# One quarter of each weight's small part, formed by an accumulating DMA in SBUF instead of a VectorE subtraction

## The chip, the cores and the metric

The kernel runs on one core of a Trainium2 chip. The time is device microseconds of that core for one execution. TensorE does the matrix products, VectorE (DVE in the rows) and ScalarE (ACT) the elementwise work, GpSimd (POOL) small chains of arithmetic, and 16 DMA engines move data; transfers are issued from the queues of SyncE (SP) and, in a few places, of GpSimd.

## The reference

Two decoder layers for 256 tokens of width 2048, in float32. Each layer is a token mixer (pooling in layer 0, sparse attention with an indexer in layer 1), a cross attention over 256 memory tokens, and a SwiGLU block; a last norm follows. What matters here is that nearly all the work is products of a [256, 2048]-like operand with weights that are read once:

```python
for i in range(DEPTH):
    x = x + mixer(rms_norm(x, norm_mix[i]))                      # pooling, or q/k/v/indexer and output products
    x = x + memory_cross_attention(rms_norm(x, norm_xattn[i]), memn, xattn_w_q[i], xattn_w_kv[i], xattn_w_o[i])
    x = x + swiglu(rms_norm(x, norm_ffn[i]), ffn_w_in[i], ffn_w_out[i])
return rms_norm(x, norm_final)

def swiglu(h, w_in, w_out):                                      # w_in 2048 x 11264, w_out 5632 x 2048
    g, u = jnp.split(h @ w_in, 2, axis=-1)
    return (jax.nn.silu(g) * u) @ w_out
```

## The kernel before, in words

**Pieces.** All weights are cut into 344 pieces of 128 partitions x 2048 columns (four of 1344), listed in `pieces` in the order in which the products use them. A piece is loaded from HBM into a `raw` tile (`load_to`, L139, on SP's queue, 1 MB), and then split into a large part `wh` and a small part `wl`, both in float32r, so that a float32 product becomes three products: `mm3` (L306 to L308) adds x_hi\*wh, x_hi\*wl and x_lo\*wh, and `mm_T` (L331, L332) is the same for results that are wanted transposed. There are three `raw` tiles and three tiles each of `wh` and `wl`.

**The split.** `split_unit` does the next 512 columns of the next piece: ScalarE copies them to `wh` with rounding (L154), and VectorE subtracts, `wl = raw - wh` (L155). A piece is thus four such units (three for the short ones).

**The order.** The program's order is written out by the code as it runs: between groups of six products the code calls `hook()`, which runs a job that is due and one or two split units. A piece may be split when at most two pieces before it are still in use (`state["cur"] + W_BUFS`), so in the steady state piece i + 2 is split while piece i is multiplied, into the tiles that piece i - 1 has just given back. The load of piece i + 2 is issued at the first split of piece i, and has to wait until the `raw` tile that it goes into has been read by the last split of piece i - 1.

**Who waits for whom.** ScalarE's first L154 of a piece waits for TensorE's last L308 of the piece three before it. L155 waits for L154. TensorE's L306 waits for L154 and L307 for L155. SP's L139 waits for the last L155 of the piece that had the tile. GpSimd has little to do: the inverse square roots of the norms (L270 to L273, seven chains of twelve instructions), six additions in the pooling mixer (L520), and the one transfer that it issues (L915).

Of the kernel before, what the change touches and what calls it, by code (L numbers as in the profile page):

```python
# [34 lines left out]
GROUPS = ((0, 4), (4, 8), (8, 11))  # L35
# pieces of the output product of the sparse attention: those of the last heads come late
AO_ORDER = [(n, j) for j in range(4) for n in range(2)] + [(n, j) for n in (2, 3) for j in range(4)]
# [3 lines left out]
NINF = -1.0e30  # L41
# 2*pi in three parts; the first two have few bits, so their multiples are exact
TPI = (6.28125, 0.0019340515136718750, 1.2556656679e-06)

# when work between products is due, in hooks: what it reads has to be there by then, or the products wait
MIX_FIRST, MIX_SPREAD = 13, 22
X_SCORES, X_SPREAD, X_MIX, X_MIX_LAST = (2, 1), (7, 5, 4, 4), 2, 5
MEM_ROW, SQ_X = 24, 12
NORM_CHUNK, NORM_POOL = (2, 3, 5), (2, 0)
RAW_BUFS, W_BUFS, BIG_BUFS, TMP_BUFS = 3, 3, 12, 8  # L50


@with_exitstack
def trunk_kernel(ctx: ExitStack, tc: tile.TileContext, a: dict, out: bass.AP):
# [20 lines left out]
    def tmp(n=512):  # L75
        """Scratch of up to 512 columns."""
        return work.tile([P, 512], F32, tag="tmp", name="tmp", bufs=TMP_BUFS)[:, :n]
# [3 lines left out]

    # ---------------------------------------------------------------- weights
    pieces = []
# [59 lines left out]
    def split_unit():  # L143
        """The next columns of the next piece, in two parts."""
        i = state["split"]
        if i >= min(len(pieces), state["cur"] + W_BUFS):
            return
        load_to(i + RAW_BUFS)
        t, w, done = raws[i]
        if not done:  # L150
            parts[i] = tuple(wpool.tile([P, 2048], F32R, tag=n, name=n) for n in ("wh", "wl"))
        c = slice(len(done) * UNIT, min((len(done) + 1) * UNIT, w))
        wh, wl = parts[i]
        A.activation(wh[:, c], t[:, c], AF.Copy)  # L154
        V.tensor_tensor(wl[:, c], t[:, c], wh[:, c].bitcast(F32), op=ALU.subtract)  # L155
        done.append(c)
        if c.stop == w:
            raws.pop(i)
            state["split"] += 1
# [11 lines left out]

    # ------------------------------------------------- work put between matmuls
    jobs, side = deque(), deque()
    made = set()

    def job(fn, delay=1, key=None):
        """fn is run by a hook, the first one that comes ``delay`` hooks from now or later and after the jobs before it."""
        jobs.append((state["hook"] + delay, fn, key))
# [7 lines left out]
    def hook():  # L186
        """Between products: a job that is due, and the next columns of weights."""
        if jobs and jobs[0][0] <= state["hook"]:
            run_job()
        if side and state["hook"] % 3 < 2:  # L190
            side.popleft()()
        split_unit()
        if state["split"] <= state["cur"] + 1:
            split_unit()
        state["hook"] += 1
# [4 lines left out]

    # -------------------------------------------------------------- constants
    gains = const.tile([P, 6, KT], F32, name="gains")
# [37 lines left out]

    # ------------------------------------------------------------------ norms
    def sumsq(dst, src, on_v=False):
# [8 lines left out]
    def rstd_of(sums, E=V, dst=None):  # L251
        """1/sqrt(sum/D + eps) of each [P, 4] of partial sums, in float32: [P, len(sums)]."""
        n = len(sums)
# [26 lines left out]

    # ------------------------------------------- transposed operands, in parts
    def split_psum(dst_h, dst_l, src):
# [11 lines left out]
    def transpose_pair(dst, src_of, kt0, gi):  # L294
        """Two k-tiles of the stationary operand: dst[:, kt % 4, hi 256 | lo 256]."""
        tp = tp_tile()
        for u in range(2):
            for t in range(2):
                T.transpose(tp[:, (2 * u + t) * P:(2 * u + t + 1) * P], src_of(kt0 + u, t), ident)  # L299
        split_pair(dst, tp, kt0, gi)  # L300

    def mm3(acc, xt, k, t, wh, wl, c0, w, first, last):
        """acc += x[:, t].T @ W for one k-tile, as hi*hi + hi*lo + lo*hi."""
        xh = xt[:, k, t * P:(t + 1) * P]
        xl = xt[:, k, S + t * P:S + (t + 1) * P]
        T.matmul(acc[:, :w], lhsT=xh, rhs=wh[:, c0:c0 + w], start=first, stop=False)  # L306
        T.matmul(acc[:, :w], lhsT=xh, rhs=wl[:, c0:c0 + w], start=False, stop=False)  # L307
        T.matmul(acc[:, :w], lhsT=xl, rhs=wh[:, c0:c0 + w], start=False, stop=last)  # L308
# [5 lines left out]
    def gemm(keys, xs, name, w=512, acc=None, at=0):  # L314
        """One chunk of w columns; xs(j) gives the four k-tiles of piece j."""
        acc = acc or [acc_tile(), acc_tile()]
# [12 lines left out]
    def mm_T(acc, wh, wl, c0, xt, k, first, last):  # L329
        """acc += (128 columns of W).T @ [x hi | x lo] for one k-tile; lo * hi goes to the half of the small terms."""  # L330
        T.matmul(acc, lhsT=wh[:, c0:c0 + P], rhs=xt[:, k, :], start=first, stop=False)  # L331
        T.matmul(acc[:, S:2 * S], lhsT=wl[:, c0:c0 + P], rhs=xt[:, k, 0:S], start=False, stop=last)  # L332

    def gemm_T(key, xs):
        """A 128-column chunk with its result transposed: [128 columns, 256 tokens] and the small terms."""
        acc = acc_tile()
        wh, wl = w_get(key)
        for kt in range(KT):
            xt = xs(kt // 4)
            mm_T(acc, wh, wl, kt * P, xt, kt % 4, kt == 0, kt == KT - 1)  # L340
            if kt % 4 == 3 and kt < KT - 1:
                hook()
        return acc
# [6 lines left out]
    class Normed:  # L350
        """x as the stationary operand of the next products: x * gain, transposed, in parts; rstd apart."""

# [5 lines left out]
        def chunk(self, n, later=0):  # L358
            """Columns 512 n of x are final."""
            def pair(u):  # L360
# [25 lines left out]

    # ------------------------------------------------- memory keys and values
    # the memory transposed, as the moving operand of k and the stationary one of v; its tokens' factors come after
    ms, mem_r, kT, vm = {}, {}, {}, {}
# [14 lines left out]
    def squares(ss, src, c):  # L404
        """Two chunks of a token half, one by each of two engines."""
        def fn():
# [13 lines left out]
    def mem_row():  # L420
        """The factors of the memory's tokens as a row, on all partitions."""
        rb = tmp(S)
# [59 lines left out]

    # ------------------------------------------------------------ pooling mixer
    # x^T times a band matrix: row t' of it holds rstd[t'] times the weight of token t' in each token's difference
    diffs = {}
# [38 lines left out]

    # --------------------------------------------------- memory cross attention
    XSC = HD ** -0.5
# [100 lines left out]

    # ------------------------------------------------------------------- SwiGLU
    def ffn(L, xn, nxt):
# [32 lines left out]
        for gi, (t0, t1) in enumerate(GROUPS):  # L662
# [3 lines left out]
            for n in range(4):  # L666
                keys = [("fo", L, ht, n) for ht in range(t0, t1)]
                if last and n == 3 and isinstance(nxt, Final):
                    # one half of the tokens after the other: the first half's end runs under the second's products
                    for t in range(2):  # L670
# [16 lines left out]

    # ------------------------------------------------------- rotary tables
    rot = big_tile(F32, (P, 2048))
# [30 lines left out]

    # --------------------------------------------------------- sparse attention
    ASC = HD ** -0.5

    def rope(dst, src, t, nh, d, rtab):
        """dst = rotated src * rstd, [P, nh * d]; the tables hold rstd."""
        c0 = 0 if d == HD else 256
# [12 lines left out]
    def sparse(xn, nxt):  # L739
# [33 lines left out]
        def to_T(dst, q0, src, key):  # L773
            """The 4 x 128 columns of src[t], transposed to dst[:, q0 + i, 256 tokens]."""
            for i in range(0, 4, 2):
# [131 lines left out]

    # ------------------------------------------------------------------ layers
    class Final:
        """The last norm: x * gain as the chunks come, the factor of each token at the end."""  # L910

# [36 lines left out]

# ------------------------------------------------------------- layout on the host
def _consts():  # L950
# [15 lines left out]
def _rows(w, n):  # L966
    """[K, N] -> [n chunks of columns, K/512, 128, 4 * N/n]: what one load brings, by partition."""
    K, N = w.shape
# [3 lines left out]
def _cols(w):  # L972
    """[2048, 512] -> [4, 128, 16 * 128]: chunks of 128 columns."""
    return w.reshape(KT, P, 4, P).transpose(2, 1, 0, 3).reshape(4, P, KT * P)
# [45 lines left out]
```

## Time and profile before

| | |
|---|---|
| time, median of 2 runs | 2006.95 us (2006.17 and 2007.72) |
| profiled execution, first to last instruction | 2005.6 us; so some 1.4 us of the median lie around it |
| TensorE: products busy / weight loads busy | 1988.5 us (99%) / 1653.2 us (82%) |
| VectorE busy | 1164.4 us (58%), 871.1 of it L155 |
| ScalarE busy | 965.5 us (48%), 768.3 of it L154 |
| GpSimd busy | 37.7 us (2%) |
| mean granted TensorE clock | 0.999 |
| DMA | 370.03 MB, SP's queue busy for 51.3% of the 16 engines' span |

The page gives no time of its own for the profiled execution beside its span of 2005.6 us; that span stands 0.07% below the median of the runs. A product's busy time is modelled and products overlap, so 99% says that TensorE always had a product in flight, not how fast they followed each other; the pitch between the starts of successive products says that. Idle time of an engine is put down to what ended last before it went on.

### The profile page before, as it was taken

The numbers are of one execution on the slowest core, as the hardware profiler recorded it, in microseconds if no ns is written. First come the engines' busy times: TensorE is split into PE (matmuls) and PEld (weight loads), VectorE is DVE, ScalarE is ACT, GpSimd is POOL, SyncE is SP. The second block draws the span as 40 slices with busy tenths as digits, with TensorE's granted clock in tenths as the row PEclk, the third lists the DMA queues.
The fourth block names the chain that finished last, engine by engine and source line by source line (L and its number), as shares of the span: only waits on it lengthen the run. The fifth ranks groups of instructions, "written<-read, shape, count | busy, mean of one in ns | idle before, by whom it ended". The sixth has DMA issues, their size and how long they took to land.

```text
span 2005.6 us, 24311 instructions
## 1 busy us (share of the span) xinstructions
PE 1988.5 (99%) x9206; PEld 1653.2 (82%) x9206; DVE 1164.4 (58%) x2217; ACT 965.5 (48%) x1936; POOL 37.7 (2%) x98
## 2 busy tenths in 40 slices
PE   8999999999999999999999999999999999999998
PEld 7888888888888888888788888888888888888886
DVE  6766655554555555556687766755555555555555
ACT  6655544444444444455455555644443444444443
POOL 1100100000000000000000000000000000000000
PEclk9999999999999999999999999999999999999999
DMA  8344555555455545545544354554555555455552
GB/s 325 142 158 170 200 197 189 175 206 196 178 189 202 195 173 194 202 168 181 170 145 168 131 188 164 189 189 173 198 197 188 189 199 191 177 207 192 189 183 111
DMA packets 53974, 370.03 MB, mean 185 GB/s; under 512 B 6368, under 2 KB 7008, under 8 KB 10208
## 3 DMA queue, kind: packets, MB, share of 16 engines
q1 hardware_dynamic: 53712, 367.43, 51.3%
q8 instruction: 72, 1.18, 0.2%
q0 software_dynamic: 144, 1.05, 0.1%
q14 instruction: 46, 0.38, 0.1%
HBM read 366.36 MB, written 2.10 MB: 184 GB/s over the span
## 4 chain that ended last, share of the span: by engine, by line
PE 99%; ACT 0%; DMA 0%; DVE 0%; issue 0%; SPq 0%; ACTq 0%
PE acc L306 29%; PE acc L308 29%; PE acc L307 29%; PE acc L331 3%; PE acc L332 1%; PE tp L299 1%; PE tp L649 1%; PE sm L794 1%; PE sm L306 0%; PE sm L307 0%; PE sm L308 0%; PE sm L838 0%; PE sm L866 0%; PE sm L574 0%; PE sm L537 0%; PE tp L858 0%
## 5 line engine op out<-in xcount | busy, mean ns | idle before, releaser
L155 DVE TENSOR_TENSOR wl<-raw,wh 128x512 fp32r<-128x512 f32 x1372 | 871.1, 687 | 473.8 <-ACT wh L154 470.2
L154 ACT ACTIVATE wh<-raw 128x512 fp32r<-128x512 f32 x1372 | 768.3, 622 | 624.0 <-PE acc L308 610.7
L306 PE MATMUL acc<-wh,big 128*128 128x512 f32 x2592 | 1027.3, 396 | 0.0
L308 PE MATMUL acc<-wh,big 128*128 128x512 f32 x2592 | 1008.4, 389 | 0.0
L307 PE MATMUL acc<-wl,big 128*128 128x512 f32 x2592 | 1006.9, 388 | 0.0
L308 PEld LDWEIGHTS acc<-wh,big 128*128 128x128 f32 x2592 | 486.4, 188 | 102.0 <-DVE big L284 0.3
L307 PEld LDWEIGHTS acc<-wl,big 128*128 128x128 f32 x2592 | 487.2, 188 | 97.4 <-DVE wl L155 1.9
L306 PEld LDWEIGHTS acc<-wh,big 128*128 128x128 f32 x2592 | 486.9, 188 | 97.1 <-issue 1.9
L639 DVE SCALAR_TENSOR_TENSOR tmp<-acc,rs,sg 128x256 f32<-128x256 f32 x88 | 42.4, 483 | 128.7 <-ACT sg L638 128.7
L638 ACT ACTIVATE sg<-acc,rs 128x256 f32<-128x256 f32 x88 | 41.6, 475 | 138.2 <-PE acc L308 138.2
L331 PE MATMUL acc<-big,wh 128*128 128x512 f32 x256 | 96.9, 417 | 1.4 <-DVE big L292 1.4
L385 DVE TENSOR_TENSOR x<-acc,x 128x512 f32<-128x512 f32 x70 | 47.4, 689 | 61.4 <-PE acc L308 61.4
L332 PE MATMUL acc<-big,wl 128*128 128x256 f32 x256 | 72.6, 284 | 0.1
L284 DVE TENSOR_TENSOR big<-tp,big 128x512 fp32r<-128x512 f32 x44 | 30.4, 692 | 62.6 <-ACT big L283 62.6
L283 ACT ACTIVATE big<-tp 128x512 fp32r<-128x512 f32 x44 | 26.3, 598 | 70.3 <-PE tp L649 70.3
L331 PEld LDWEIGHTS acc<-big,wh 128*128 128x128 f32 x256 | 49.0, 191 | 12.6 <-ACT wh L154 1.2
L292 DVE SCALAR_TENSOR_TENSOR big<-tp,gains,big 128x256 fp32r<-128x256 f32 x96 | 41.9, 478 | 26.3 <-ACT big L290 25.6
L290 ACT ACTIVATE big<-tp,gains 128x256 fp32r<-128x256 f32 x96 | 40.3, 475 | 34.3 <-PE tp L299 22.3
L332 PEld LDWEIGHTS acc<-big,wl 128*128 128x128 f32 x256 | 49.2, 192 | 1.0 <-DVE wl L155 0.6
L249 ACT ACTIVATE junk<-x 128x512 f32<-128x512 f32 x52 | 33.1, 637 | 20.5 <-DVE x L385 11.4
L847 ACT ACTIVATE tmp<-tmp,mx 128x128 f32<-128x128 f32 (+1 forms) x32 | 14.3, 448 | 40.2 <-DVE mx L845 40.2
L270 POOL TENSOR_TENSOR rs<-rs 128x2 f32<-128x2 f32 x21 | 8.3, 396 | 1198.7 <-DVE rs L265 1197.6
(143 smaller groups left out, 621.1 us busy)
## 6 DMA issues: line engine op xcount, KB each, us to landing
raw<-in_fi SPq DMA_DIRECT2D x176, 1024.0 KB, 4.8
raw<-in_fo SPq DMA_DIRECT2D x88, 1024.0 KB, 4.8
raw<-in_wq SPq DMA_DIRECT2D x16, 1024.0 KB, 4.9
raw<-in_wao SPq DMA_DIRECT2D x16, 1024.0 KB, 4.9
raw<-in_xv SPq DMA_DIRECT2D x8, 1024.0 KB, 5.4
raw<-in_xq SPq DMA_DIRECT2D x8, 1024.0 KB, 4.7
raw<-in_xo SPq DMA_DIRECT2D x8, 1024.0 KB, 4.7
raw<-in_wqi SPq DMA_DIRECT2D x8, 1024.0 KB, 4.9
```

The costliest lines, as they stand in the source:

```text
L154: A.activation(wh[:, c], t[:, c], AF.Copy)
L155: V.tensor_tensor(wl[:, c], t[:, c], wh[:, c].bitcast(F32), op=ALU.subtract)
L290: A.activation(dst_h, src, AF.Copy, scale=g)
L292: V.scalar_tensor_tensor(dst_l, src, g, dst_h.bitcast(F32), op0=ALU.mult, op1=ALU.subtract)
L306: T.matmul(acc[:, :w], lhsT=xh, rhs=wh[:, c0:c0 + w], start=first, stop=False)
L307: T.matmul(acc[:, :w], lhsT=xh, rhs=wl[:, c0:c0 + w], start=False, stop=False)
L308: T.matmul(acc[:, :w], lhsT=xl, rhs=wh[:, c0:c0 + w], start=False, stop=last)
L331: T.matmul(acc, lhsT=wh[:, c0:c0 + P], rhs=xt[:, k, :], start=first, stop=False)
L332: T.matmul(acc[:, S:2 * S], lhsT=wl[:, c0:c0 + P], rhs=xt[:, k, 0:S], start=False, stop=last)
L385: V.tensor_tensor(xc, acc[t], xc, op=ALU.add)
L638: A.activation(sg, acc[t][:, 0:S], AF.Silu, scale=r[:, t:t + 1])
L639: V.scalar_tensor_tensor(h[:, t, :], acc[t][:, S:2 * S], r[:, t:t + 1], sg, op0=ALU.mult, op1=ALU.mult)
```

## The change

For every piece from the 13th on (`BY_DMA_FROM = 12`), the first unit of 512 columns no longer goes through VectorE. ScalarE writes `wh` as before and then a second time from `raw` into `wl`, with the sign turned (so `wl = -wh`); then GpSimd issues a transfer from `raw` to `wl` in SBUF that adds what it reads to what is there, so that `wl = raw - wh`. The other units, and the first twelve pieces, are as before. The line numbers of the changed kernel are higher by two before this place and by seven after it (L139 is L141, L306 to L308 are L313 to L315, L332 is L339). Other lines of the diff take comments away.

```diff
+BY_DMA_FROM = 12
...
         A.activation(wh[:, c], t[:, c], AF.Copy)
-        V.tensor_tensor(wl[:, c], t[:, c], wh[:, c].bitcast(F32), op=ALU.subtract)
+        if len(done) == 0 and i >= BY_DMA_FROM:
+
+            A.activation(wl[:, c], t[:, c], AF.Copy, scale=-1.0)
+            nc.gpsimd.dma_start(wl[:, c], t[:, c], accum_op=ALU.add)
+        else:
+            V.tensor_tensor(wl[:, c], t[:, c], wh[:, c].bitcast(F32), op=ALU.subtract)
```

ScalarE, in the first SwiGLU block, around one pair of activations (`sg`) and the split of a result (`big`). Before:

```order
L638 ACTIVATE sg<-acc,rs 128x256 x2
L154 ACTIVATE wh<-raw 128x512 x2
L283 ACTIVATE big<-tp 128x2x256
L154 ACTIVATE wh<-raw 128x512 x14
L638 ACTIVATE sg<-acc,rs 128x256 x2
```

The same place with the change:

```order
L645 ACTIVATE sg<-acc,rs 128x256 x2
L156 ACTIVATE wh<-raw 128x512 x2
L159 ACTIVATE wl<-raw 128x512
L290 ACTIVATE big<-tp 128x2x256
L156 ACTIVATE wh<-raw 128x512 x4
L159 ACTIVATE wl<-raw 128x512
L156 ACTIVATE wh<-raw 128x512 x4
L159 ACTIVATE wl<-raw 128x512
L156 ACTIVATE wh<-raw 128x512 x4
L159 ACTIVATE wl<-raw 128x512
L156 ACTIVATE wh<-raw 128x512 x2
L645 ACTIVATE sg<-acc,rs 128x256 x2
```

Sixteen copies of ScalarE between two pairs of activations become twenty: one more behind the first unit of each piece, ahead of the other three.

GpSimd, at the end of the norm ahead of that block and behind it, with what each instruction waits for (DMASW are counts of transfers that GpSimd issued, DMAHW of SP's loads). Before, one norm's chain follows the other:

```order
L272 TENSOR_SCALAR rs<-rs 128x2 [waits Pool_49]
L273 TENSOR_TENSOR rs<-rs 128x2 [waits Pool_49]
L270 TENSOR_TENSOR rs<-rs 128x2 [waits DVE_49]
L271 TENSOR_TENSOR rs<-rs 128x2 [waits Pool_49]
L272 TENSOR_SCALAR rs<-rs 128x2 [waits Pool_49]
```

With the change transfers stand between:

```order
L279 TENSOR_SCALAR rs<-rs 128x2 [waits Pool_49]
L280 TENSOR_TENSOR rs<-rs 128x2 [waits Pool_49]
L160 DMA wl<-raw 128x512 [waits DMASW0_49,DMAHW4_49,PE_49,Activation_49]
L160 DMA wl<-raw 128x512 [waits DMASW1_49,DMAHW5_49,PE_49,Activation_49]
L160 DMA wl<-raw 128x512 [waits DMASW2_49,DMAHW6_49,PE_49,Activation_49]
L160 DMA wl<-raw 128x512 [waits DMASW3_49,DVE_49,DMAHW7_49,PE_49,Activation_49]
```

Each such transfer waits for ScalarE's copy of the same columns; the DMASW count it waits for is that of the transfer that wrote the same `wl` tile three pieces earlier.

TensorE, at the border of two pieces in that block: the last products of one, and the first of the next (L306 and L307). Before:

```order
L306 MATMUL acc<-wh,big 128x512 [waits Activation_49]
L307 MATMUL acc<-wl,big 128x512 [waits DVE_49]
L308 MATMUL acc<-wh,big 128x512
L306 MATMUL acc<-wh,big 128x512
L307 MATMUL acc<-wl,big 128x512
L308 MATMUL acc<-wh,big 128x512
L306 MATMUL acc<-wh,big 128x512 [waits Activation_49]
L307 MATMUL acc<-wl,big 128x512 [waits DVE_49]
```

With the change:

```order
L313 MATMUL acc<-wh,big 128x512 [waits Activation_49]
L314 MATMUL acc<-wl,big 128x512 [waits DVE_49]
L315 MATMUL acc<-wh,big 128x512
L313 MATMUL acc<-wh,big 128x512
L314 MATMUL acc<-wl,big 128x512
L315 MATMUL acc<-wh,big 128x512
L313 MATMUL acc<-wh,big 128x512 [waits Activation_49]
L314 MATMUL acc<-wl,big 128x512 [waits DMASW6_49]
```

The first product of a piece that reads `wl` now waits for the transfer to land. In the same way SP's load into a `raw` tile (L141) now waits for that tile's transfer as well as for its last subtraction.

## Rows read from the trace of the kernel before

**Rows 1.** The page: busy time, share of the span and instructions of each engine.

```profile
PE 1988.5 (99%) x9206; PEld 1653.2 (82%) x9206; DVE 1164.4 (58%) x2217; ACT 965.5 (48%) x1936; POOL 37.7 (2%) x98
```

**Rows 2.** The page: the chain that ended last.

```profile
PE 99%; ACT 0%; DMA 0%; DVE 0%; issue 0%; SPq 0%; ACTq 0%
```

**Rows 3.** Waits of the whole span: engine line <- releaser: us in total, times, longest.

```profile
ACT wh L154 <- PE acc L308: 610.7, 229, 6.2
...
PE tp L299 <- DMA big<-in_mem: 5.7, 2, 4.5
...
PEld acc L307 <- DVE wl L155: 1.9, 8, 0.2
```

**Rows 4.** Groups by line: line engine op tiles shapes xcount | busy us, mean ns | idle before.

```profile
L155 DVE TENSOR_TENSOR wl<-raw,wh 128x512 fp32r<-128x512 f32 x1372 | 871.1, 687 | 473.8 <-ACT wh L154 470.2
L154 ACT ACTIVATE wh<-raw 128x512 fp32r<-128x512 f32 x1372 | 768.3, 622 | 624.0 <-PE acc L308 610.7 <-issue 5.3 <-DMA raw<-in_xv 3.2
L307 PEld LDWEIGHTS acc<-wl,big 128*128 128x128 f32 x2592 | 487.2, 188 | 97.4 <-DVE wl L155 1.9
```

**Rows 5.** Stretches: PE, PEld, DVE, ACT, POOL busy (instructions), PEclk, DMA share, GB/s.

```profile
300.00:700.00 400.00, 400.00 (x1790) 331.10 (x1789) 207.93 (x338) 176.74 (x327) 0.00 (x0) 1.00 0.53 190
...
1000.00:1250.00 250.00, 250.00 (x1225) 208.10 (x1224) 176.43 (x454) 135.28 (x319) 3.85 (x13) 1.00 0.45 159
```

**Rows 6.** Timeline, TensorE weight loads in a SwiGLU block: start us, us, engine line.

```profile
566.61 0.19 PEld L307 LDWEIGHTS acc<-wl,big 128*128 128x128 f32 x1
566.83 0.19 PEld L308 LDWEIGHTS acc<-wh,big 128*128 128x128 f32 x1
567.06 0.19 PEld L306 LDWEIGHTS acc<-wh,big 128*128 128x128 f32 x1
567.29 0.19 PEld L307 LDWEIGHTS acc<-wl,big 128*128 128x128 f32 x1
```

**Rows 7.** Timeline, ScalarE in the same block [idle before <- releaser].

```profile
562.04 2.20 ACT L154 ACTIVATE wh<-raw 128x512 fp32r<-128x512 f32 x4 [3.24 <-PE acc L308]
567.48 1.68 ACT L154 ACTIVATE wh<-raw 128x512 fp32r<-128x512 f32 x3 [3.24 <-PE acc L308]
...
578.86 2.20 ACT L154 ACTIVATE wh<-raw 128x512 fp32r<-128x512 f32 x4 [0.61 <-PE acc L308]
584.30 2.20 ACT L154 ACTIVATE wh<-raw 128x512 fp32r<-128x512 f32 x4 [3.24 <-PE acc L308]
```

**Rows 8.** DMA: queue, packets, MB, share of 16 engines; below, issues and median us to landing.

```profile
q1 hardware_dynamic: 53712, 367.43, 51.3%
...
raw<-in_fi SPq DMA_DIRECT2D x176, 1024.0 KB, 4.8
raw<-in_fo SPq DMA_DIRECT2D x88, 1024.0 KB, 4.8
...
big<-in_mem SPq DMA_DIRECT2D x8, 256.0 KB, 7.7
...
big<-in_pool_scale SPq DMA_DIRECT2D x1, 1024.0 KB, 10.4
big<-in_norm_final POOLq DMA_DIRECT2D x1, 1024.0 KB, 4.7
out_x<-big SPq DMA_DIRECT2D x4, 192.0 KB, 2.3
```

**Rows 9.** DMA from 0 to 12 us, where most packets are of 2 KB.

```profile
q1 hardware_dynamic: 1409, 3.03, 77.9%
```

**Rows 10.** Timeline, GpSimd issuing its one transfer.

```profile
1221.85 0.74 POOL L915 DMA_DIRECT2D big<-in_norm_final  x1 [0.34 <-issue]
```

**Rows 11.** DMA from 1221 to 1227 us: busy tenths in 40 slices of 0.15 us.

```profile
DMA  0000000000000009699999798999989511000049
...
q0 software_dynamic: 144, 1.05, 42.7%
```

**Rows 12.** Timeline, ScalarE: third piece of the first SwiGLU block; the last pieces.

```profile
203.92 0.53 ACT L712 ACTIVATE tmp<-tmp 128x384 f32<-128x384 f32 x1 [5.25 <-DVE tmp L711]
204.35 0.61 ACT L154 ACTIVATE wh<-raw 128x512 fp32r<-128x512 f32 x1
...
1980.89 2.70 ACT L154 ACTIVATE wh<-raw 128x512 fp32r<-128x512 f32 x5
```

**Rows 13.** Timeline, TensorE: the first reads of wl of those two pieces.

```profile
207.89 0.19 PEld L307 LDWEIGHTS acc<-wl,big 128*128 128x128 f32 x1
...
1984.70 0.19 PEld L307 LDWEIGHTS acc<-wl,big 128*128 128x128 f32 x1
```

**Rows 14.** Waits of SP's queue.

```profile
SPq L139 <- DVE wl L155: 1723.1, 328, 11.6
```

## The prediction

> **What bounds the kernel now.** I read the busy shares first. TensorE has a product in flight for 1988.5 of 2005.6 us; VectorE stands at 58%, ScalarE at 48%, GpSimd at 2% [rows 1]. The chain that ended last is TensorE for 99% [rows 2]. So the question for any edit on another engine is whether TensorE waits for it. The table of waits answers: over the whole span TensorE's weight loads waited for VectorE's subtraction eight times, 1.9 us together [rows 3]. The other way round, VectorE idles 473.8 us ahead of its subtractions, nearly all of it for ScalarE's copy, and ScalarE idles 624.0 us ahead of its copies, nearly all of it for TensorE's last read of the old piece [rows 4]. The splitting engines are paced by TensorE, not it by them.
>
> That 99% alone would not prove it, since busy products overlap. So I looked at the pitch: weight loads of a SwiGLU block start 0.22 to 0.23 us apart, three of them in 0.68 us, in an unbroken series [rows 6]. 24 products make a piece, 5.44 us, and ScalarE's bursts of copies confirm it: each burst starts when TensorE gives a piece back, at 562.04 and 567.48, at 578.86 and 584.30 [rows 7]. In the long stretch from 300 to 700 us the clock is granted in full and VectorE is half idle [rows 5]. In the sparse attention, its densest stretch, VectorE is at 176.43 of 250 us and TensorE still has no gap [rows 5]. I conclude that TensorE's own rate is the bound.
>
> A page of the Trainium skill, "Perfetto Trace Analysis", section "Identifying the Most-Contended Engine", calls busy products a bad metric and would have me judge headroom by the busy share of weight loads, here 82%. If that headroom were to be had, it would speak for a larger gain; it is the third rival below.
>
> **What the change removes.** 344 pieces less 12 are 332, so 332 subtractions of 687 ns leave VectorE [rows 4]: 228 us, from 1164 to 936 us busy (47%). TensorE waited 1.9 us for all 1372 of them, so this gives back at most 2 us; I count it as nothing. VectorE's freed time has no other taker.
>
> **What it adds on ScalarE.** 332 copies of 622 ns [rows 4]: 207 us, from 965 to 1172 us (58%). They are hidden in ScalarE's wait for TensorE: in the steady block a burst of four copies lasts 2.20 us of 5.44, with 3.24 us of idle time ahead of the next [rows 7]; five last 2.8. If that cover were gone, each would delay the following units of its piece by 0.6 us. Nothing there reads these units before two pieces later.
>
> **What it adds on GpSimd.** 332 transfers. The only one it issues now keeps it for 740 ns [rows 10]; 332 of these are 246 us on an engine with 38 us of work [rows 1]. In front of a transfer GpSimd waits for ScalarE, and queued behind it are the norms' chains of small instructions. ScalarE runs that copy as soon as TensorE frees the tile, so the wait is part of one piece; a chain may be a few us late, and its result is wanted by activations, not by a product directly. I take nothing.
>
> **The new wait.** This is what decides. TensorE's first read of `wl` in a piece, and SP's load into the `raw` tile, now wait for the transfer to land. Let D be the time from GpSimd's issue to the landing. The steady path: TensorE frees a `wl` tile; ScalarE copies twice (1.24 us); D; then TensorE must read. With three tiles it reads two pieces after the release, 2 x 5.44 = 10.88 us [rows 7]. So D may be up to about 9.5 us at no cost.
>
> How long is D? No row shows an accumulating transfer inside SBUF, so I build it up. GpSimd's one transfer starts at 1221.85 [rows 10] and the first packet moves in slice 16, at 1221 + 15 x 0.15 = 1223.25 [rows 11]: 1.4 us ahead of the data. Its data ends about 1226, some 0.5 us before its landing at 4.7 us [rows 8, 11]. The data: between 0 and 12 us, where the mean packet has 2.15 KB (3.03 MB in 1409), they take 77.9% of 16 engines x 12 us, 106 ns each [rows 9]. The new transfer has 128 rows of 2 KB, eight for each engine: 0.85 us if it were a plain copy. It reads two streams and adds, so I take twice that, 1.7 us; once is the lower end, four times (3.4 us) the upper. Beside it SP's loads keep the engines busy for 51.3% [rows 8], and one load is 128 packets of 306 ns (51.3% of 16 x 2005.6 us over 53712) on 16 engines, 2.45 us; on average half of it is in the way, 1.2 us. D = 1.4 + 1.7 + 1.2 + 0.5 = 4.8 us. The bounds from whole rows: 2.3 us, the landing of a 192 KB store, and 10.4 us, the slowest load of the crowded start, where 256 KB ones took 7.7 [rows 8]. I take 4.8, which lies beside the two nearest rows, GpSimd's own issue (4.7 us) and the loads in the same traffic (4.8 us) [rows 8]; both ends stay for the range.
>
> The page "DMA: Bandwidth & Descriptors" of the Trainium skill, section "Anatomy of one DMA — SWDGE (gpsimd) path", gives 2.0 us plus the bytes at 436 GB/s for a transfer issued by GpSimd, an estimate of 2.6 us for these 256 KB. By that the two places below would cost 0.6 us in all, not 5.2; its 4.4 us for 1 MB agrees with the 4.7 us of the row, but it says nothing of adding.
>
> **Where D = 4.8 us is still too long.** Two places have less room. In the first SwiGLU block ScalarE sits 5.25 us behind the rotary tables, and the third piece is copied late, from 204.35 to 204.96; TensorE reads its small part at 207.89 [rows 12, 13]: 2.93 us of room for 0.62 + 4.8, so TensorE stands for 2.5 us. The pieces behind it are late as well, but TensorE is then late by the same. And the last piece: of the five copies from 1980.89 the second is its first unit, ended at about 1982.03 (0.52 us after the first starts, 0.62 long), read at 1984.70 [rows 12, 13]: 2.67 us of room, 2.7 us short. Sum: 2.5 + 2.7 = 5.2 us.
>
> **The loads.** SP waits for the last subtraction before it reloads a tile, 328 times [rows 14]. That comes about 2.5 us after the first copy; the transfer lands 0.62 + 4.8 after it, so a load starts 3 us later. It takes 4.8 us [rows 8] and ScalarE reads it three pieces (16.3 us) after the release that began the split: 0.6 + 5.4 + 4.8 is under 11, so 5 us are left. In all the engines' share goes from 51% by 332 x 1.7 / 2005.6 = 28% to 79%. I take nothing; the bound is the second rival.
>
> **Sum.** Against the profiled execution: 2005.6 + 5.2 = 2010.8 us; with the 1.4 us that lie between it and the median, 2012 us, against 2006.95. Its own range is 2005 (D = 2.3) to 2040 (D near 9, where other pieces with less than the steady room come in).
>
> **The rivals.** *The landing is too late (slower).* If an accumulating transfer takes longer than 9.5 us, each piece waits. A `wl` tile then goes round in one piece of use and X = 0.1 + 1.24 + D of filling; with three tiles the piece takes X / 2. At D = 12 that is 6.67 instead of 5.44 us, and with the 264 SwiGLU pieces [rows 8] alone 325 us: about 2330 us. For it speaks that no row has a DMA engine adding, and the 10.4 us of the start; against it, that this landing is of a crowd of loads at once. It decides from D of about 9.5 us. Chance 0.14.
>
> *The DMA engines fill up (slower).* If adding costs four times a plain packet, 3.4 x 332 = 1129 us, 56%, the share is 107%, and the time 1.07 x 2005.6, about 2150 us. It decides from 2.9 us per transfer, where 51.3 + 48 reach the whole. Against it: that is 3.4 times the plain packets. Chance 0.12.
>
> *TensorE has hidden headroom (faster).* A weight load takes 188 ns [rows 4] of a pitch of 227 [rows 6]; if VectorE's traffic were what stretches the pitch and all of it went, 2005.6 x 0.83, about 1660 us, would remain. (This is what the rule of "Perfetto Trace Analysis" would make of the 82%.) But TensorE keeps that pitch in a block where VectorE is half idle, and the rows name 1.9 us of waits [rows 3]. Chance 0.01 of over 2%.
>
> *It makes no difference at all:* D is under 3 us, and VectorE's relief pays the rest, 2006 us. It lies in the forecast's case.
>
> **How the numbers follow.** Forecast's case 0.73, slower rivals 0.26, faster 0.01. 2% (40 us) is about what tells a change of this kernel from none, and the forecast's case lies within it. Range: from 2003 to 2200 us, so that it takes in the filled engines and the landing up to D of about 11; what is left out is the rest of the late landing and the faster case, under 0.15.
>
> **What would show it.** Right: GpSimd's 332 issues near 0.74 us each; L160 landing within 4 to 7 us; TensorE still at 99%, with waits for the transfer in a handful of places, the third SwiGLU piece and the last piece first, 2 to 3 us each; VectorE near 936 and ScalarE near 1172 us; the DMA share near 80%. Wrong: TensorE's reads of `wl` (L314) waiting for the transfer hundreds of times (late landing), or loads landing much later than 4.8 us and ScalarE waiting for `raw` (full engines).

## The result

The changed kernel takes 2024.41 us (median of 2 runs, 2024.00 and 2024.83) against 2006.95: a ratio of 1.0087, 95% interval 1.0071 to 1.0103. It is 17.5 us slower, less than 2% and clear of the noise. Forecast were 2012 us, 5 us slower.

The page of the changed kernel gives busy times, DMA queues, the chain and three groups (line engine op, out<-in, xcount | busy, mean ns | idle before, releaser):

```profile
span 2022.2 us, 25606 instructions
...
PE 1994.1 (99%) x9206; PEld 1654.4 (82%) x9206; DVE 969.0 (48%) x1885; ACT 1137.7 (56%) x2268; POOL 317.9 (16%) x430
...
q1 hardware_dynamic: 53712, 367.43, 54.0%
q0 software_dynamic: 47952, 88.10, 25.4%
...
PE 94%; ACT 2%; DMA 1%; issue 1%; DVE 1%; POOL 0%; SPq 0%; ACTq 0%; POOLq 0%
...
L162 DVE TENSOR_TENSOR wl<-raw,wh 128x512 fp32r<-128x512 f32 (+1 forms) x1040 | 671.8, 688 | 662.0 <-ACT wh L156 659.2
...
L160 POOL DMA_DIRECT2D wl<-raw x332 | 286.3, 866 | 1581.5 <-ACT wl L159 1315.8
L159 ACT ACTIVATE wl<-raw 128x512 fp32r<-128x512 f32 x332 | 205.0, 617 | 0.0
...
raw<-in_fi SPq DMA_DIRECT2D x176, 1024.0 KB, 5.9
...
wl<-raw POOLq DMA_DIRECT2D x332, 256.0 KB, 5.6
```

The work has moved as the diff says: VectorE 1164 to 969 us, ScalarE 965 to 1138, GpSimd 38 to 318 [rows 1], DMA engines at 54.0 + 25.4 = 79.4% (51.3% before [rows 8]). TensorE is still busy for 99%, but the chain of work that ended last is no longer TensorE's alone: 94%, was 99% [rows 2]. Its waits (engine line <- releaser: total us, times, longest):

```profile
PEld acc L314 <- DMA wl<-raw: 13.2, 7, 6.1
...
PE acc L314 <- DMA wl<-raw: 10.4, 6, 5.7
```

There are seven standstills for the new transfer, 13.2 us in all. Of the eight short waits for VectorE (1.9 us [rows 3]) four are left, 1.0 us. (The two rows tell of the same waits, once for the weight load and once for the product; they don't add.) In the steady block nothing has changed for TensorE:

```profile
300.00:700.00 400.00, 400.00 (x1790) 331.12 (x1789) 167.22 (x269) 215.63 (x403) 62.01 (x72) 1.00 0.85 239
```

It starts 1790 products there, as before [rows 5], beside a DMA share of 0.85.

**Where the 16.6 us of the span went.** I set the first read of `wl` of each piece against that in the trace of before. The steps in the difference of over 0.5 us from the 13th piece on: second to fifth piece of the first SwiGLU block +0.7, +1.2, +6.0, +1.8; 14th piece +0.5; around the indexer +1.5 and +0.8; start of the second SwiGLU block +0.7; seventh piece from the end +1.8; last piece +1.4. These ten make 16.4. The largest come first, at the third to fifth SwiGLU pieces; these are TensorE's weight loads:

```profile
210.54 0.19 PEld L314 LDWEIGHTS acc<-wl,big 128*128 128x128 f32 x1 [1.26 <-DMA wl<-raw]
...
221.95 0.29 PEld L314 LDWEIGHTS acc<-wl,big 128*128 128x128 f32 x1 [6.09 <-DMA wl<-raw]
...
229.16 0.19 PEld L314 LDWEIGHTS acc<-wl,big 128*128 128x128 f32 x1
```

The read at 210.54 is that at 207.89 before [rows 13]. Why the fourth piece stood for 6 us is seen on ScalarE and in GpSimd's queue:

```profile
211.55 0.63 ACT L159 ACTIVATE wl<-raw 128x512 fp32r<-128x512 f32 x1
```

```profile
207.20 0.86 POOL L160 DMA_DIRECT2D wl<-raw  x1 [11.50 <-ACT wl L159]
212.78 0.69 POOL L277 TENSOR_TENSOR rs<-rs 128x2 f32<-128x2 f32 x1 [4.72 <-DVE rs L272]
...
217.98 0.20 POOL L280 TENSOR_TENSOR rs<-rs 128x2 f32<-128x2 f32 x1
218.54 2.68 POOL L160 DMA_DIRECT2D wl<-raw  x3 [0.36 <-ACT wh L156]
```

The copy that the transfer waits for ended at 212.2. The transfer was issued at 218.54, 6.4 us later, because a norm's chain of twelve small instructions stood ahead of it, and that chain had waited for VectorE until 212.78 (until 210.83 in the kernel before). The transfer landed at 221.9; three of them were issued one after the other behind the chain. And the standstill had an echo, in the granted clock (PEclk, third column from the end) of the stretches in it and behind it:

```profile
216.00:222.00 6.00, 0.33 (x3) 0.05 (x1) 2.56 (x5) 2.53 (x5) 4.45 (x9) 0.76 0.36 61
222.00:226.00 4.00, 4.00 (x10) 3.13 (x11) 0.00 (x0) 0.00 (x0) 0.00 (x0) 0.50 1.08 231
226.00:230.00 4.00, 4.00 (x19) 3.32 (x18) 0.00 (x0) 1.28 (x1) 0.00 (x0) 1.00 0.95 395
```

For some 4 us TensorE ran at the lower of its two levels (0.50, 1.2 GHz), 10 products where the next 4 us have 19. That is the +1.8 at the fifth piece, whose own transfer was there long before.

The second kind is a late landing. The seventh piece from the end was issued at once and landed 9.0 us later, at 1972.82. One load of 1 MB moved beside it (issued at 1963.17, landed at 1971.58), and from 1967.25 on the next piece's transfer (GpSimd's row, and TensorE's):

```profile
1963.77 0.86 POOL L160 DMA_DIRECT2D wl<-raw  x1 [4.57 <-ACT wl L159]
```

```profile
1972.86 0.19 PEld L314 LDWEIGHTS acc<-wl,big 128*128 128x128 f32 x1 [1.85 <-DMA wl<-raw]
```

Over all 332 the time from issue to landing is 3.2 us at least, 5.6 in the median and 9.1 at most.

### The profile page after: what moved, and what is told of

It reads as the page before. It is cut to its first block, busy times and chain, and to the rows that moved or that the text cites. A ratio compares the mean times of both kernels' runs of the same rounds, so it can differ in the third digit from the quotient of the medians.

```text
span 2022.2 us, 25606 instructions
## 1 busy us (share of the span) xinstructions
PE 1994.1 (99%) x9206; PEld 1654.4 (82%) x9206; DVE 969.0 (48%) x1885; ACT 1137.7 (56%) x2268; POOL 317.9 (16%) x430
## 3 DMA queue, kind: packets, MB, share of 16 engines
q0 software_dynamic: 47952, 88.10, 25.4%
## 4 chain that ended last, share of the span: by engine, by line
PE 94%; ACT 2%; DMA 1%; issue 1%; DVE 1%; POOL 0%; SPq 0%; ACTq 0%; POOLq 0%
PE acc L314 28%; PE acc L315 28%; PE acc L313 28%; PE acc L338 3%; PE acc L339 1%; DMA wl<-raw 1%; PE tp L656 1%; PE tp L306 1%; ACT big L297 1%; PE sm L801 1%; ACT junk L256 0%; PE sm L313 0%; PE sm L315 0%; PE sm L314 0%; PE sm L845 0%
## 5 line engine op out<-in xcount | busy, mean ns | idle before, releaser
L156 ACT ACTIVATE wh<-raw 128x512 fp32r<-128x512 f32 x1372 | 792.5, 622 | 530.7 <-PE acc L315 513.4
L313 PE MATMUL acc<-wh,big 128*128 128x512 f32 x2592 | 1028.1, 397 | 0.0
L314 PE MATMUL acc<-wl,big 128*128 128x512 f32 x2592 | 1008.5, 389 | 10.4 <-DMA wl<-raw 10.4
L315 PE MATMUL acc<-wh,big 128*128 128x512 f32 x2592 | 1009.2, 389 | 0.0
L162 DVE TENSOR_TENSOR wl<-raw,wh 128x512 fp32r<-128x512 f32 (+1 forms) x1040 | 671.8, 688 | 662.0 <-ACT wh L156 659.2
L314 PEld LDWEIGHTS acc<-wl,big 128*128 128x128 f32 x2592 | 487.8, 188 | 111.0 <-DMA wl<-raw 13.2
L315 PEld LDWEIGHTS acc<-wh,big 128*128 128x128 f32 x2592 | 486.9, 188 | 101.9 <-DVE big L291 0.3
L313 PEld LDWEIGHTS acc<-wh,big 128*128 128x128 f32 x2592 | 487.3, 188 | 97.2 <-issue 1.9
L160 POOL DMA_DIRECT2D wl<-raw x332 | 286.3, 866 | 1581.5 <-ACT wl L159 1315.8
L159 ACT ACTIVATE wl<-raw 128x512 fp32r<-128x512 f32 x332 | 205.0, 617 | 0.0
L339 PE MATMUL acc<-big,wl 128*128 128x256 f32 x256 | 72.8, 284 | 0.1
L339 PEld LDWEIGHTS acc<-big,wl 128*128 128x128 f32 x256 | 49.4, 193 | 1.0 <-DVE wl L162 0.6
```

The costliest lines, as they stand in the source:

```text
L159: A.activation(wl[:, c], t[:, c], AF.Copy, scale=-1.0)
L160: nc.gpsimd.dma_start(wl[:, c], t[:, c], accum_op=ALU.add)
```

## The experiments

In each, `...` stands for the changed kernel's other lines.

**e1, the norms' chains on VectorE.** This takes the chain out of GpSimd's queue.

```diff
-            self.rstd = rstd_of([self.ss[:, t, :] for t in range(2)], nc.gpsimd)
+            self.rstd = rstd_of([self.ss[:, t, :] for t in range(2)])
```

> The changed kernel, with the norms' chain of twelve small instructions moved from GpSimd to VectorE, so that no transfer stands behind it in GpSimd's queue. In the changed kernel the transfer of the fourth SwiGLU piece was issued 6.4 us after its copy on ScalarE had ended, behind such a chain, and TensorE stood 6 us for it and then ran for 3.8 us at half the pitch. Theory A (GpSimd's queue): that standstill, the 1.8 us at half the clock behind it and the 1.5 us at the first indexer piece go: 2024.4 - 9 = about 2015 us. Theory B (the transfer itself lands too late, because loads are in its way): the queue costs nothing of its own, 2022 to 2025 us.

Measured: 2022.74 us (1.0075, 1.0063 to 1.0088), 1.7 us less, within the spread of its own runs (2020.4 to 2024.1). Theory A alone falls. The fourth piece shows why (GpSimd, then TensorE):

```profile
212.49 0.86 POOL L160 DMA_DIRECT2D wl<-raw  x1 [4.40 <-DVE rs L268]
```

```profile
219.24 0.79 PE L314 MATMUL acc<-wl,big 128*128 128x512 f32 x1 [2.94 <-DMA wl<-raw]
```

The transfer was issued 6 us earlier and landed only 2.7 us earlier: now it shared the engines with a load and took 6.7 us instead of 3.4. TensorE stood 3.4 us by the weight load's row, and the lower clock followed here too, 11 products in 4 us:

```profile
220.00:224.00 4.00, 4.00 (x11) 3.13 (x10) 1.03 (x2) 1.50 (x2) 0.33 (x1) 0.50 0.92 247
```

It cost another 2.7 us (an estimate from the starts of the products, against the trace of before), so this place lost 6.0 us instead of 7.8. Around the indexer the loss did not go either: without the chain another piece waited there, 1.6 us, for a transfer that took 6.7 us to land.

**e1c, the same edit on the kernel before**, as control.

> The kernel before with only the norms' chains moved from GpSimd to VectorE, as a control for e1 and e8: the move by itself should neither cost nor gain, 2005 to 2009 us.

Measured: 2006.79 us (1.0000, 0.9991 to 1.0009). The move is free.

**e2, eleven pieces back to VectorE.**

```diff
+LATE = (29, 30, 31, 162, 164, 167, 213, 215, 337, 340, 343)
...
-        if len(done) == 0 and i >= BY_DMA_FROM:
+        if len(done) == 0 and i >= BY_DMA_FROM and i not in LATE:
```

> The changed kernel, but in eleven of the 332 pieces (those before which TensorE stood in its trace, or had under 0.1 us left: three of the first SwiGLU block, three around the indexer, two of the second block, the last three where it stood) VectorE forms the small part as before. Theory C (all of the loss is in these few places, the other 321 transfers are free): within 2 us of the kernel before, 2006 to 2009 us. Rival (the loss is spread: DMA traffic or ScalarE's extra copies slow everything a little, and the standstills only gather it): at least 2014 us.

Measured: 2012.43 us (1.0027, 1.0018 to 1.0037), between the two forecasts: 12 of 17 us are in these pieces, but the standstills that remain (4.9 us in four) are at other pieces, mostly their neighbours: +1.5 at the fifth SwiGLU piece, +2.2 and +0.6 around the indexer, +0.6 late in the second SwiGLU block. Behind the one of 2.2 us the granted clock fell (third column from the end), and another 1.5 us went (an estimate from the starts of the products, against the trace of before):

```profile
946.00:949.00 3.00, 3.00 (x12) 3.00 (x11) 1.92 (x5) 0.34 (x1) 0.00 (x0) 0.50 0.88 311
```

It is the stretch that is tight, not the piece.

**e3, ScalarE's copy without the transfer.**

```diff
             A.activation(wl[:, c], t[:, c], AF.Copy, scale=-1.0)
-            nc.gpsimd.dma_start(wl[:, c], t[:, c], accum_op=ALU.add)
-        else:
-            V.tensor_tensor(wl[:, c], t[:, c], wh[:, c].bitcast(F32), op=ALU.subtract)
+        V.tensor_tensor(wl[:, c], t[:, c], wh[:, c].bitcast(F32), op=ALU.subtract)
```

> The changed kernel with ScalarE's extra copy, but without the transfer; VectorE forms the whole small part as before, over that copy. It prices the extra 205 us of ScalarE alone. Theories A to C: ScalarE's copies are hidden, 2006 to 2009 us (at most the third and fourth SwiGLU pieces, copied late behind the rotary tables, cost 1 to 2 us). Rival (ScalarE's extra work is what makes the tight pieces late): 2012 us or more.

Measured: 2009.29 us (1.0011, 1.0002 to 1.0020). This is just above the range. 332 copies, for which ScalarE is busy 171 us longer (1136.8 us against 965.5), cost some 2 us: 0.5 at the 14th piece and 0.75 each at the second piece of both SwiGLU blocks, steps that the changed kernel shows too.

**e4, the transfers into a tile that no engine reads**; all small parts by VectorE.

```diff
+    un = const.tile([P, 512], F32R, name="un")
...
-            A.activation(wl[:, c], t[:, c], AF.Copy, scale=-1.0)
-            nc.gpsimd.dma_start(wl[:, c], t[:, c], accum_op=ALU.add)
-        else:
...
+            nc.gpsimd.dma_start(un, t[:, c], accum_op=ALU.add)
+        V.tensor_tensor(wl[:, c], t[:, c], wh[:, c].bitcast(F32), op=ALU.subtract)
```

> The kernel before, with all of the small part by VectorE, and beside it the same 332 accumulating transfers of 256 KB from the raw tile, but into one tile that no engine reads (its sums are thrown away; there is one scratch tile fewer for the rest). The traffic, and SP's wait for the transfer before it reloads a raw tile, are there; TensorE's wait for the landing is not, nor is ScalarE's copy. Theory C: nothing is lost without TensorE's wait, 2006 to 2009 us. Rival (full DMA engines make the loads late): loads land 1 us later as in the changed kernel and TensorE waits for ScalarE or VectorE instead, 2012 us or more.

Measured: 2509.47 us (1.2500, 1.2483 to 1.2517). A mistake in the design: with one tile each transfer has to wait for the one before, as GpSimd's queue shows.

```profile
706.63 0.86 POOL L159 DMA_DIRECT2D un<-raw  x1 [6.38 <-DMA un<-raw]
713.85 0.86 POOL L159 DMA_DIRECT2D un<-raw  x1 [6.36 <-DMA un<-raw]
720.84 0.86 POOL L159 DMA_DIRECT2D un<-raw  x1 [6.13 <-DMA un<-raw]
```

One in 7.1 us, where a piece takes 5.44, and SP's loads wait for them. It does give a price for the rival of the late landing: with a round 1.7 us longer than a piece, the kernel lost 502 us, 1.5 us for each of the 332 pieces.

**e4b, the same with two such tiles in turn.**

```diff
+            nc.gpsimd.dma_start(un[i % 2], t[:, c], accum_op=ALU.add)
```

> As e4_unread (all small parts by VectorE, the 332 transfers into tiles that no engine reads, SP's reload still waiting for them), but the transfers go in turn into two such tiles, so that each waits for the landing of the last but one and not of the last; two scratch tiles fewer for the rest. In e4 each transfer waited for the one before (2053 us in total, 6.9 us from issue to landing), so its 2509 us were that chain of 332 x 7 us and not the traffic. Theory C (the traffic alone costs nothing): 2006 to 2011 us. Rival (the traffic makes loads late): 2020 us or more.

Measured: 2008.20 us (1.0005, 0.9996 to 1.0014). The whole traffic is there (GpSimd's queue 25.6% of the engines' span, loads landing after 6.1 us instead of 4.8), and the loss is not clear of the noise: without TensorE's wait the traffic is free. (These transfers wait for the load of their piece and not for ScalarE's copy, so their timing is not quite that of the changed kernel.)

**e5, two units of each piece by the transfer.**

```diff
-        if len(done) == 0 and i >= BY_DMA_FROM:
+        if len(done) < 2 and i >= BY_DMA_FROM:
```

> The changed kernel with the first two units of each piece (1024 columns) by the transfer, twice the traffic: GpSimd's queue took 25.3% of the DMA engines' span for one unit, SP's loads 51 to 54%. By these rows two units fill them: 54 + 51 = 105% of 2022 us, at least 2110 us, and more where they wait in turn. Rival (the engines are not the limit, only the few tight places count twice): 2040 us or less.

Measured: 2183.96 us (1.0882, 1.0867 to 1.0897). The engines are full, as in the stretch from 300 to 700 us, where the DMA share (last column but one) is 1.01 and TensorE starts 1645 products instead of 1790. ScalarE waits for loads, TensorE for transfers:

```profile
300.00:700.00 400.00, 378.57 (x1645) 302.68 (x1643) 111.41 (x180) 232.13 (x436) 114.36 (x133) 1.00 1.01 261
```

```profile
ACT wh L156 <- DMA raw<-in_fi: 334.6, 137, 6.8
...
PEld acc L314 <- DMA wl<-raw: 169.7, 143, 4.3
```

**e6, the transfer in the steady parts of the SwiGLU blocks only** (241 pieces).

```diff
-        if len(done) == 0 and i >= BY_DMA_FROM:
+        if len(done) == 0 and (35 <= i < 160 or 218 <= i < 334):
```

> The changed kernel with the transfer only in the steady parts of the two SwiGLU blocks (241 of the 332 pieces), and VectorE as before around the cross attention, the sparse attention, the start of each SwiGLU block and the end. In e2, where eleven pieces went back to VectorE, their neighbours came late instead and 5 us stayed. Theory D (a steady piece has room enough and costs nothing; the loss belongs to the stretches in which ScalarE's copies come late): 2006 to 2009 us. Rival (a small loss on every piece): 2012 us or more.

Measured: 2008.38 us (1.0007, 0.9998 to 1.0016), with one wait of 0.7 us for a transfer (0.3 us in the product's row). That wait is for the longest landing of this run, 9.4 us, issued at 1578.46, so the steady room of about 9.5 us stands and is nearly used up. Theory D holds, and no faster kernel comes of it: 143 us less on VectorE buy nothing.

**e9, the other 91 pieces only.**

```diff
-        if len(done) == 0 and i >= BY_DMA_FROM:
+        if len(done) == 0 and (12 <= i < 35 or 160 <= i < 218 or i >= 334):
```

> The complement of e6: the transfer only in the 91 pieces that e6 left to VectorE (cross attentions, sparse attention, the starts of the SwiGLU blocks, the last ten pieces). Theory D: these hold the whole loss, 2021 to 2025 us. Rival (the loss needs the traffic of all 332): under 2016 us.

Measured: 2022.82 us (1.0083, 1.0069 to 1.0097): 16.1 of the 17.5 us with 27% of the transfers; the rest is within the intervals. The places are not quite the same: the two standstills around the indexer come one piece earlier and are longer (1.9 and 1.6 us), and that at the seventh piece from the end is gone. Which pieces of a tight stretch come late differs between these kernels.

**e7, half of each load.**

```diff
-                c = slice(c, c + UNIT if i == 0 else w)
+                c = slice(c, c + UNIT if i == 0 else w if i < 12 else min(w, 1024))
...
-        A.activation(wh[:, c], t[:, c], AF.Copy)
+        r = c if i < 12 or c.start < 1024 else slice(c.start - 1024, c.stop - 1024)
+        A.activation(wh[:, c], t[:, r], AF.Copy)
...
-            V.tensor_tensor(wl[:, c], t[:, c], wh[:, c].bitcast(F32), op=ALU.subtract)
+            V.tensor_tensor(wl[:, c], t[:, r], wh[:, c].bitcast(F32), op=ALU.subtract)
```

> The changed kernel with only the first 1024 columns of each piece from the 13th on loaded (the other half is split from these columns again, so half of the weights is left out of the result). All instructions of the engines are as in the changed kernel, the loads bring 0.5 MB. Theory B (the landing is late because a load is in its way): the median from issue to landing falls from 5.6 us to below 4.5, TensorE's waits for it from 24 us (both rows of the table together) to under half, and the time to 2010 to 2015 us. Theory A (GpSimd's queue, ScalarE's lateness): 2020 us or more.

Measured: 2020.45 us (1.0068, 1.0055 to 1.0081). The landing falls to 4.0 us in the median and 7.0 at most, the standstills around the indexer shrink to 0.5 us in one place, that at the seventh piece from the end is gone; but the fourth SwiGLU piece still stands 6.3 us behind the chain. Theory B alone falls too. (The time is in the range named for theory A, but A alone fell with e1. My expectation added the two rows of waits, which tell of the same time.)

**e8, both edits, e1 and e7.**

> Both edits of e1 and e7 together: norms' chains on VectorE and half of each load from the 13th piece on (half of the weights is left out of the result). Alone they gave back 1.7 and 4 of the 17 us, because with the chain gone the fourth SwiGLU piece still waits for a transfer that lands 6.8 us after its issue, and with short landings it still stands behind the chain. Theory E (two causes in a row at the same place, each of which covers the other): together they give back more than the sum, the 6.2 us standstill of e7 and its half clock go, 2010 to 2014 us. Rival (independent small losses): the sum, 2018 to 2019 us.

Measured: 2012.81 us (1.0030, 1.0019 to 1.0042), 11.6 us less than the changed kernel, where the two alone gave 1.7 and 4.0. Theory E holds: taking the chain away gives 1.7 us beside whole loads and 7.6 beside half loads. The fourth piece waits 0.9 us in the product's row (1.4 in the weight load's), since its transfer now lands 4.7 us after its issue instead of the 6.7 of e1, and no half clock follows:

```profile
212.03 0.86 POOL L161 DMA_DIRECT2D wl<-raw  x1 [4.40 <-DVE rs L269]
```

```profile
216.78 0.50 PE L315 MATMUL acc<-wl,big 128*128 128x512 f32 x1 [0.93 <-DMA wl<-raw]
```

What stays, some 6 us, is this wait, the two places that were forecast (1.3 and 1.5 us) and the 2 us of ScalarE's copies.

## Why the prediction held, and where it was off

The result lies in the forecast's case, which was wide; the loss is three times the 5.2 us of the sum. The two places in that sum gave 2.7 us of the 16.6, so the sum itself did not find most of the loss.

- **The bound.** Right: TensorE's pitch, and so nothing for VectorE's relief. e6 shows it.
- **What is removed and added.** Right in count. VectorE lost 195 us and ScalarE gained 172, not 228 and 207: I took counts times the mean of one, but instructions back to back overlap in these rows (871.1 us busy for 1372 x 687 = 943 [rows 4]). ScalarE's copies, counted as hidden, are not quite free: 2 us (e3).
- **D.** 4.8 us forecast, 5.6 measured. The engines' part was well taken: 25.3% of 16 x 2022.2 us over 332 transfers is 24.7 us, 1.54 on each of 16 engines (1.7 forecast). GpSimd takes 0.87 us for an issue, not 0.74. What is larger is the loads' part: D is 3.2 us at least, and with half-size loads (e7) 4.0 in the median; beside whole loads it goes up to 9.1. I took half a load on average, 1.2 us; the median, 5.6 less 3.2, says 2.4. (The 306 ns for a load's packet was low as well: it averages in small packets, and the page before counts 10208 of 53974 under 8 KB.) A wait is decided by the worst case at the tight place, not by the average.
- **The two tight places.** Both stood, with 1.3 and 1.5 us instead of 2.5 and 2.7: no load was in their way, and D was 3.3 and 3.2, not 4.8. (For a D of 2.6 us the prediction's own rooms give 0.8 us at the two places, not 0.6.)
- **The step that failed** is that on GpSimd's queue, "I take nothing". I asked who waits behind a transfer, and not what a transfer waits behind: the norm's chain, which in turn starts when VectorE has done its part. At the fourth SwiGLU piece TensorE stood 6.0 us behind it, with the clock 7.8. The chain is one of two causes there: without it alone (e1) the place still lost 6.0 us to a landing beside a load and the clock, and only with both taken away (e8) 1.3. The clock's fall behind that standstill was in no term either. The sentence that the pieces behind the third are late but TensorE by the same failed there too: the fourth was later by more.
- **The rest**, 4 us around the indexer and at the seventh piece from the end, is landings of 7.7 and 9.0 us and, at the indexer's first piece, again the chain (its transfer was issued 3.2 us late); the bound of 10.4 us covered them, the sum did not.
- **The rivals.** The engines fill up, but only with twice the transfers (e5). The late landing came to 9.1 us, just short of the 9.5 from which the steady piece would have paid. TensorE's hidden headroom did not show: with a fifth less VectorE work from 300 to 700 us (e6: 165.59 us busy, not 207.93) TensorE starts 1791 products there, as before. A kernel with none of VectorE's traffic was not tried.

## What to carry to other kernels

A queue is followed in both directions: a transfer put on an engine with 2% of work stands behind that work, and its few chains may sit just where the pieces are late. Slack is read at the tightest stretch and set against the longest landing beside the loads, not the median; e6 and e9 show the same edit free in 241 pieces and costly in 91. Two causes at one place hide each other, so take both away before calling either harmless.

## What the runs showed of the hardware

An accumulating transfer of 128 rows of 2 KB inside SBUF takes 3.2 us from issue to landing with no load beside it, and 1.54 us of each DMA engine, 171 ns for a packet (25.3% of 16 x 2022.2 us over 332 x 144), against 106 ns for the packets of the start, 2.15 KB in the mean [rows 9]. The Trainium skill's "DMA: Bandwidth & Descriptors", section "Anatomy of one DMA — SWDGE (gpsimd) path", would give 2.6 us for a transfer of these bytes (an estimate from its fit, which says nothing of adding); the least that is measured with the addition is 0.6 us above, the median more than twice as much. Behind a standstill of its products of 5.7 us TensorE ran at a granted clock of 0.50 (1.2 GHz) for some 4 us, and so it did behind the 2.9 us of e1 (11 products from 220 to 224 us) and the 1.9 us of e2 (12 products of 336 columns from 946 to 949 us); behind the 0.9 us of e8 and the 1.4 us at the seventh piece from the end here it kept the full clock. And a transfer that shares the engines with a load landed twice as late at the fourth SwiGLU piece: 6.7 us (e1) instead of 3.4.
